# Down products of a gated feed-forward block: from plain block products to seven products of 2x2 blocks

## The chip, the cores and the metric

The kernel runs on one core of a Trainium2 chip. The metric is the device time of one execution, in microseconds (us). The engines are TensorE (PE, with its weight loads as PEld), VectorE (DVE), ScalarE (ACT), GpSimd (POOL) and SyncE (SP); SP and POOL start the DMAs. Each engine works through its own queue in order, and waits for others by semaphores.

## The reference

One inference step of a decoder of two layers, for 512 prompt tokens and 8 sample tokens that share the weights. Each layer has a feed-forward half-step, a mixer, and another half-step:

```
x = x + 1/2 * SwiGLU_a(RMSNorm(x))
x = x + Mixer(RMSNorm(x))       # layer 0: differential attention + gated linear attention; layer 1: mLSTM
x = x + 1/2 * SwiGLU_b(RMSNorm(x))
SwiGLU(x) = (silu(x @ w_gate) * (x @ w_up)) @ w_down      # 1024 -> 2816 -> 1024, all float32
```

So there are four half-steps, and the product with w_down in them is what is changed. The mixers' caches and states are outputs too; they are computed as before.

## The kernel before

The activations x lie feature by feature: 8 tiles of 128 features, each with 520 token columns, cut into two chunks, c0 of 256 and c1 of 264 columns (`CH`). A float32 product is made of three products of the faster type fp32r: `split` (L103) makes the high part by a cast on ACT (L105) and the low part by a subtraction on DVE (L106), and `dense` (L93) multiplies high weights by high x (L100), high by low x (L101) and low by high x (L102), for each block of 128x128 weights. Three matmuls per block and chunk, then.

The kernel is a row of stages: half-step, even mixer, half-step, half-step, odd mixer, half-step. `half_step` (L259) works through 2816 / 128 = 22 hidden tiles in GROUPS of 8, 7 and 7.

- The first four tiles (LEAD, function `early`, tiles g and u) are computed plainly while the norm and the combinations of x are still being made.
- The other 18 gate and up tiles use seven products of 2x2 blocks in place of eight (`product`): the 2x2 blocks are gate and up against the two halves of the 8 input tiles on the side of the weights, and the halves against the two chunks on the side of x. The products are p1, q5, p4 of the tile before, q6, p2, p3, p7, in that order, 4 blocks x 3 = 12 matmuls each, so 84 per tile. p1, q6, p7, p4 run into bank A, p2 into B, q5 and p3 into E. In between ACT evicts partial sums and DVE adds and multiplies them (L473 c<-B, L482 v<-E, L485 c<-A, L486, L490 c<-A). The results are split into hh and hl.
- The weights of such a tile come by SP in the tiles graw, u and raw (s); POOL adds blocks of w to s by an accumulating DMA (L426), and DVE adds graw and raw twice (L436). Then whi (ACT) and wlo (DVE) are made.
- At the end of a group its hidden tiles hh, hl are multiplied plainly by w_down: for each of 8 output tiles d and both chunks, the group's 8 or 7 blocks x 3 matmuls into a bank y, and DVE adds y to x (L558).
- In the last group of a half-step the last four d are taken chunk by chunk (lag = 4): four y of c0, then four y of c1, and between these the sum of squares (ACT sq, DVE acc, PE ss, DVE rs, PE bc) for the next stage's norm is put. The next stage's first products (pj in a mixer, g and u in a half-step) come behind them.

The order in each queue is fixed when the program is built, by a scheduler of the tile framework that takes the program's order and the priorities of marked blocks (`high_priority(AHF)`, for the weights). Pools of buffers decide the rest: three raw, two graw, one u2, five whi and wlo of the wide kind and two of the narrow kind, six PSUM banks.

Of the kernel before, what the change touches and what calls it, by code (L numbers as in the profile page):

```python
# [7 lines left out]
F32 = mybir.dt.float32  # L8
# [14 lines left out]
GROUPS = (8, 7, 7)  # L23
# [19 lines left out]
def ffn_order():  # L43

    out, f0 = [], 0
    for n in GROUPS:
        fs = range(f0, f0 + n)
        f0 += n
        for f in fs:
            out += [("g", f, k) for k in range(KT)] + [("u", f, k) for k in (4, 5, 6, 7, 0, 1, 2, 3)]  # L50
        for d in range(KT):
            out += [("d", d, f) for f in fs]
    return out


class Net:
# [101 lines left out]
    def norm_apply(self, c, ks, bc=None):  # L158
# [6 lines left out]
        for k in ks:  # L165
            q = self.tmp.tile([P, 264], F32, tag="xt", name="xt", bufs=3)
# [92 lines left out]
    def half_step(self, pos, first, last, xp, hp, pa):  # L259
# [122 lines left out]
        def early(f, w, c):  # L382
# [8 lines left out]
            h = f.h[:, s:s + n]  # L391
            if first:
                r = rms[c]
                v = small("v")[:, :n]
# [8 lines left out]
        def unit(u, gate):  # L403
            raw = (hp.tile([P, UNIT * P], F32, tag="graw", name="graw", bufs=2) if gate else
                   self.wraw.tile([P, UNIT * P], F32, tag="raw", name="raw"))
            self.wq.dma_start(out=raw, in_=self.t["w"][u])
            return raw

        def parts(src, n, names):

            tag = "" if n == 2 else "u"
            hi = self.whl.tile([P, n * H * P], F32R, tag=f"whi{tag}", name="whi", bufs=None if n == 2 else 2)
            lo = self.whl.tile([P, n * H * P], F32R, tag=f"wlo{tag}", name="wlo", bufs=None if n == 2 else 2)
            self.split(hi, lo, src)
            return {name: [(hi[:, i * P:i * P + P], lo[:, i * P:i * P + P]) for i in range(b * H, b * H + H)]
                    for b, name in enumerate(names)}

        def weights_gate(f):

            B = H * P  # L420
            f.g = unit(f.u0, True)
            f.u = hp.tile([P, B], F32, tag="u2", name="u2")
            self.wq.dma_start(out=f.u, in_=self.t["w"][f.u0 + 1, :, :B])
            f.s = self.wraw.tile([P, 2, B], F32, tag="raw", name="raw")
            self.wq.dma_start(out=f.s, in_=self.t["w"][f.u0 + 1, :, None, B:].to_broadcast([P, 2, B]))
            nc.gpsimd.dma_start(out=f.s, in_=self.t["w"][f.u0:f.u0 + 2, :, :B].rearrange("u p c -> p u c"),  # L426
                                accum_op=ALU.add)
            with tc.high_priority(AHF):
                f.w = parts(f.g, 2, ("g1", "g2"))

        def weights_rest(f):
            B = H * P
            g1, g2, s1 = f.g[:, :B], f.g[:, B:], f.s[:, 1, :]
# [3 lines left out]
            with tc.high_priority(AHF):  # L437
                f.w |= parts(f.u, 1, ("u2",))
                f.w |= parts(f.s.rearrange("p u c -> p (u c)"), 2, ("s3", "s1"))
                add(g1, s1)  # L440
                add(g2, g1)
                f.w |= parts(f.g, 2, ("s2", "s4"))

        class Hidden:
            def __init__(self, u0):
                self.u0 = u0
# [4 lines left out]
        def small(name):  # L451
            return hp.tile([P, n1], F32, tag=name, name=name, bufs=2)

        def product(kind, f, j):
            w, v = {"p1": ("g1", "x11"), "p2": ("g2", "x21"), "q5": ("s1", "a"), "q6": ("s2", "b"),
                    "p7": ("s3", "c"), "p3": ("s4", "x22"), "p4": ("u2", "d")}[kind]
            n = n0 if kind in ("p1", "p2", "p4") else n1
            new = kind in ("p1", "p2", "q5")
            if kind == "p1":
                f.A = bank("A")  # L460
            elif kind == "p2":
                f.B = bank("B")
            elif kind == "q5":
                f.E = bank("E")
            ps = f.B if kind == "p2" else f.E if kind in ("q5", "p3") else f.A
            self.dense(ps[:, :n], f.w[w], lambda k: tuple(q[:, :n] for q in ops[v](k)), ends=(new, True),
                       open_=kind != "p2")
            if kind == "p1":
                f.c1 = small("c1")
                self.evict(f.c1[:, :n0], ps[:, :n0])  # L470
            elif kind == "p2":
                g = f.c1[:, :n0]
                nc.vector.tensor_tensor(out=g, in0=ps[:, :n0], in1=g, op=ALU.add)  # L473
                nc.scalar.activation(g, g, AF.Silu)
            elif kind == "q5":
                f.c5 = small("c5")
                self.evict(f.c5, ps[:, :n1])
            elif kind == "q6":
                f.v = small("v")
                self.evict(f.v, ps[:, :n1])  # L480
            elif kind == "p3":
                nc.vector.tensor_tensor(out=f.v, in0=ps[:, :n1], in1=f.v, op=ALU.add)  # L482
                nc.scalar.activation(f.v, f.v, AF.Silu)
            elif kind == "p7":
                nc.vector.tensor_tensor(out=f.c5, in0=ps[:, :n1], in1=f.c5, op=ALU.add)  # L485
                nc.vector.tensor_tensor(out=f.v, in0=f.v, in1=f.c5, op=ALU.mult)  # L486
                self.split(hh[:, j, late], hl[:, j, late], f.v)
            elif kind == "p4":
                g = f.c1[:, :n0]
                nc.vector.tensor_tensor(out=g, in0=ps[:, :n0], in1=g, op=ALU.mult)  # L490
                self.split(hh[:, j, :n0], hl[:, j, :n0], g)
            step()

        u0 = pos // UNIT
        groups = []
        for nf in GROUPS:
            groups.append([Hidden(u0 + 2 * j) for j in range(nf)])
            u0 += 3 * nf
        leads = groups[0][:LEAD]
# [7 lines left out]
        while i < LEAD:  # L507
# [4 lines left out]
            for f in fs:  # L512
                f.h = hp.tile([P, T], F32, tag="h", name="h", bufs=LEAD)
# [9 lines left out]
        for gi, (nf, fs) in enumerate(zip(GROUPS, groups)):  # L523
            order = []
            for j in range(LEAD if gi == 0 else 0, nf):
                order += [("gate", j), ("rest", j), ("p1", j), ("q5", j)] + [("p4", j - 1)] * (j > (LEAD if gi == 0 else 0))
                order += [("q6", j), ("p2", j), ("p3", j), ("p7", j)]
            order.append(("p4", nf - 1))
            hh = hl = None
            for kind, j in order:  # L530
                if hh is None and kind in ("p7", "p4"):
                    hh = hp.tile([P, max(GROUPS), T], F32R, tag="hh", name="hh")
                    hl = hp.tile([P, max(GROUPS), T], F32R, tag="hl", name="hl")
                    if gi == 0:
# [1330 lines left out]
```

## Time and profile before

| | |
|---|---|
| time of the kernel before | 2206.93 us, median of 3 runs (2199.34 to 2207.18) |
| profiled execution | 2204.89 us, of it 2203.0 us from the first to the last instruction |
| mean granted clock of TensorE | 0.993 of full speed |
| busy: PE, PEld, DVE, ACT, POOL | 2157.5, 2044.5, 1418.3, 1015.2, 132.6 us |
| matmuls | 18340 |

Busy time is the union of the records of an engine. Matmuls overlap in the array, so that a record (some 0.28 us) says how long one takes, and the step from start to start how many go through in a time. A name such as y stands for all buffers of that name; `out<-in` gives what an instruction writes and reads, then its shape.

### The profile page before, as it was taken

Reading aid. Unit: us, or ns where it says so; the run is one execution under the profiler, and the core shown is the slowest. Engines: PE = TensorE matmul, PEld = TensorE weight load, DVE = VectorE, ACT = ScalarE, POOL = GpSimd, SP = SyncE. Lnnn points to the kernel's source line nnn. Section 1 sums busy time; section 2 is a strip of 40 time slices with the busy share of each in tenths; the row PEclk is TensorE's granted clock in tenths of the full one; section 3 lists DMA queues with packets and bytes.
Section 4 is the critical chain, followed back from the end, with each engine's and each line's share of the span. In section 5 each row is a group of like instructions: output and inputs, shape, how many; then the busy total and the mean of one; then the engine's idle time right before and its main releaser. Section 6 shows DMA issues by size and latency. Waiting matters only on the chain. (4 is left out here: it accounts for less than half of the span.)

```text
span 2203.0 us, 45950 instructions
## 1 busy us (share of the span) xinstructions
PE 2157.5 (98%) x18340; PEld 2044.5 (93%) x18340; DVE 1418.3 (64%) x3017; ACT 1015.2 (46%) x1932; POOL 132.6 (6%) x184
## 2 busy tenths in 40 slices
PE   8999999999999999999999999999999899999999
PEld 8999999876777899999999999999899899999999
DVE  8847475544486687475767566667655688648473
ACT  6636263334523455263645444454555555526261
POOL 1010101000000100101000000100000000000000
PEclk9999999999999999999999999999999999999999
DMA  7455544577787754555634555632545565555552
GB/s 226 138 127 166 135 134 140 161 262 260 237 274 240 258 145 141 123 170 124 175 97 120 156 141 150 149 100 89 159 149 158 151 194 171 143 130 158 144 135 78
DMA packets 146188, 352.94 MB, mean 160 GB/s; under 512 B 14433, under 2 KB 19090, under 8 KB 145846
## 3 DMA queue, kind: packets, MB, share of 16 engines
q1 hardware_dynamic: 113088, 273.79, 38.6%
q0 software_dynamic: 27120, 63.18, 14.5%
q10 hardware_dynamic: 5766, 13.05, 1.6%
q8 instruction: 144, 2.36, 0.4%
q14 instruction: 70, 0.57, 0.1%
HBM read 332.84 MB, written 17.11 MB: 159 GB/s over the span
## 5 line engine op out<-in xcount | busy, mean ns | idle before, releaser
L105 ACT CAST whi<-raw 128x1024 fp32r<-128x1024 f32 (+1 forms) x368 | 307.8, 840 | 345.6 <-PE y L101 178.9
L106 DVE TENSOR_TENSOR wlo<-raw,whi 128x1024 fp32r<-128x1024 f32 (+1 forms) x368 | 354.1, 967 | 145.9 <-ACT whi L105 139.9
L101 PE MATMUL y<-hl,whi 128*128 128x256 f32 (+1 forms) x1408 | 398.0, 283 | 0.0
L100 PE MATMUL y<-hh,whi 128*128 128x256 f32 (+1 forms) x1408 | 397.1, 283 | 0.0
L102 PE MATMUL y<-hh,wlo 128*128 128x256 f32 (+1 forms) x1408 | 396.9, 282 | 0.0
L100 PE MATMUL pj<-xh,whi 128*128 128x264 f32 (+1 forms) x896 | 261.2, 292 | 4.9 <-ACT whi L105 2.0
L101 PEld LDWEIGHTS y<-hl,whi 128*128 128x128 f32 x1408 | 265.1, 188 | 0.1
L100 PEld LDWEIGHTS y<-hh,whi 128*128 128x128 f32 x1408 | 264.8, 188 | 0.3
L102 PEld LDWEIGHTS y<-hh,wlo 128*128 128x128 f32 x1408 | 264.8, 188 | 0.0
L101 PE MATMUL pj<-xl,whi 128*128 128x264 f32 (+1 forms) x896 | 255.9, 286 | 0.0
L102 PE MATMUL pj<-xh,wlo 128*128 128x264 f32 (+1 forms) x896 | 255.2, 285 | 0.1
L101 PE MATMUL A<-xb,whi 128*128 128x264 f32 (+1 forms) x864 | 246.0, 285 | 0.0
L100 PE MATMUL A<-xb,whi 128*128 128x264 f32 (+1 forms) x864 | 244.8, 283 | 0.0
L102 PE MATMUL A<-xb,wlo 128*128 128x264 f32 (+1 forms) x864 | 244.7, 283 | 0.0
L105 ACT CAST whi<-graw 128x1024 fp32r<-128x1024 f32 x144 | 151.2, 1050 | 194.8 <-PE y L101 108.9
L106 DVE TENSOR_TENSOR wlo<-graw,whi 128x1024 fp32r<-128x1024 f32 x144 | 176.0, 1222 | 56.8 <-ACT whi L105 56.8
L558 DVE SCALAR_TENSOR_TENSOR x<-y,x 128x256 f32<-128x256 f32 (+1 forms) x192 | 81.9, 427 | 201.1 <-PE y L102 200.5
L100 PEld LDWEIGHTS pj<-xh,whi 128*128 128x128 f32 x896 | 170.8, 191 | 20.0 <-issue 9.1
L101 PEld LDWEIGHTS pj<-xl,whi 128*128 128x128 f32 x896 | 170.9, 191 | 3.4 <-issue 3.3
L102 PEld LDWEIGHTS pj<-xh,wlo 128*128 128x128 f32 x896 | 170.6, 191 | 1.9 <-issue 1.4
L100 PE MATMUL E<-xh,whi 128*128 128x264 f32 x576 | 163.8, 284 | 0.5 <-ACT c L586 0.5
L100 PEld LDWEIGHTS A<-xb,whi 128*128 128x128 f32 x864 | 162.7, 188 | 1.3
(469 smaller groups left out, 5168.2 us busy)
## 6 DMA issues: line engine op xcount, KB each, us to landing
raw<-w SPq DMA_DIRECT2D x240, 512.0 KB, 3.7
raw<-w POOLq DMA_DIRECT2D x112, 512.0 KB, 6.0
graw<-w SPq DMA_DIRECT2D x72, 512.0 KB, 4.8
kt<-ckt SPq DMA_DIRECT2D x128, 256.0 KB, 4.6
vtile<-cv SPq DMA_DIRECT2D x128, 256.0 KB, 4.2
u<-w SPq DMA_DIRECT2D x72, 256.0 KB, 3.0
cs<-sc SPq DMA_DIRECT2D x16, 512.0 KB, 5.3
kb<-kqd SPq DMA_DIRECT2D x16, 512.0 KB, 6.9
```

The costliest lines, as they stand in the source:

```text
L100: nc.tensor.matmul(ps, lhsT=wh, rhs=xh, start=(ends[0] and i == ks[0]), stop=False, skip_group_check=open_)
L101: nc.tensor.matmul(ps, lhsT=wh, rhs=xl, start=False, stop=False, skip_group_check=open_)
L102: nc.tensor.matmul(ps, lhsT=wl, rhs=xh, start=False, stop=(ends[1] and i == ks[-1]), skip_group_check=open_)
L105: self.nc.scalar.copy(out=hi, in_=src)
L106: self.nc.vector.tensor_tensor(out=lo, in0=src, in1=hi, op=ALU.subtract)
L558: nc.vector.scalar_tensor_tensor(xs, y[:, :n], -0.5, xs, ALU.mult, ALU.add)
```

## The change

GROUPS becomes 6, 6, 6 and 4. The down products of the first three groups, 18 of the 22 tiles, are now also made with seven products of 2x2 blocks; the last group of 4 stays plain. A `Down` is such a unit. Its blocks are: pairs of hidden tiles (three pairs in a group, the sum over k), pairs of outputs (d and d + 4) and the two chunks. So a group has 4 Downs, of 7 products x 3 pairs x 3 = 63 matmuls. Their weights come and are combined as those of a gate tile, in sizes of 768 and 384 columns instead of 1024 and 512. Each product that ends a partial sum is added to x by DVE (L552), six additions per Down: two of E (264 columns), two of A (264), one of A and one of B (256).

A pair of hidden tiles is gathered in a tile `h` of four slots of 264 columns (tag stg, one buffer; the second pair of leads lies in a graw buffer), whose unused last 8 columns POOL sets to zero. When both tiles are there, `combine` makes the differences (L468 of 528 columns, L471 and L472 of 264) and splits all seven operands into hh and hl (792, 528 and 528 columns).

The Downs of a group don't stand at its end: they come behind the first gate tile of the next group. And p1 of a unit is now copied by ACT from bank A to bank B, where p2 adds to it, in place of the addition c<-B on DVE. Buffers: squares sq 4 to 3, xt 3 to 2, c5 2 to 1.

```diff
-GROUPS = (8, 7, 7)
+GROUPS = (6, 6, 6, 4)
...
+        class Pair:
+            def open(self, tag="stg"):
+                if self.h is None:
+                    self.h = hp.tile([P, 4 * n1], F32, tag=tag, name="h",
+                                     bufs=2 if tag == "graw" else None).rearrange("p (s t) -> p s t", s=4)
+                    nc.gpsimd.memset(self.h[:, 0:3:2, n0:], 0.0)
...
+            def parts(self, a, b, j):
+                self_split(hidden[0][:, self.i, j:j + b - a], hidden[1][:, self.i, j:j + b - a], self.h[:, a:b])
+
+            def combine(self):
+                x11, x22, x21, x12 = [self.h[:, i] for i in range(4)]
+                cm = hp.tile([P, 4 * n1], F32, tag="cmb", name="cmb").rearrange("p (s t) -> p s t", s=4)
+                nc.vector.tensor_tensor(out=cm[:, 0:2], in0=self.h[:, 0:2], op=ALU.subtract,
+                                        in1=x12[:, None, :].to_broadcast([P, 2, n1]))
+                self.parts(0, 3, 0)
+                nc.vector.scalar_tensor_tensor(cm[:, 2], cm[:, 1], -1.0, x11, ALU.mult, ALU.subtract)
+                nc.vector.scalar_tensor_tensor(cm[:, 3], cm[:, 2], -1.0, x21, ALU.mult, ALU.subtract)
+                for a in (0, 2):
+                    self_split(hidden[0][:, self.i, 3 + a:5 + a], hidden[1][:, self.i, 3 + a:5 + a], cm[:, a:a + 2])
...
+        class Unit:
+            def product(f, kind):
+                w, v = WHERE[kind]
+                n = n0 if kind in ("p1", "p2", "p4") else n1
+                if kind == "p1":
+                    f.A, f.B = bank("A"), bank("B")
+                elif kind == "q5":
+                    f.E = bank("E")
+                ps = f.B if kind == "p2" else f.E if kind in ("q5", "p3") else f.A
+                self.dense(ps[:, :n], f.w[w], lambda k: tuple(q[:, :n] for q in f.rhs(v, k)), ends=(kind in ("p1", "q5"), True),
+                           open_=True)
+                if kind == "p1":
+                    self.evict(f.B[:, :n0], ps[:, :n0])
+                f.out(kind, ps[:, :n])
+                step()
...
+        class Down(Unit):
...
+            def out(f, kind, ps):
+                if kind == "p1":
+                    return
+                row = 0 if kind in ("q6", "p2", "p3") else 1
+                cols = slice(0, n0) if kind in ("p2", "p4") else late
+                xs = x[:, f.d + row * H, cols]
+                nc.vector.scalar_tensor_tensor(xs, ps, row - 0.5, xs, ALU.mult, ALU.add)
...
+                seq += fs[:1] + downs + fs[1:]
...
+        for f in seq:
+            weights(f)
+            f.product("p1")
+            f.product("q5")
+            if before is None:
...
+                for p in (leads[0].pair, leads[2].pair):
+                    p.combine()
+            else:
+                before.product("p4")
...
+            for kind in ("q6", "p2", "p3", "p7"):
+                f.product(kind)
+            before = f
+        before.product("p4")
```

How this stands in the queues, at three places. First VectorE where the first down products of the kernel begin. Before, the last gate tile of the first group (c, v, hl) is followed by updates x<-y with a low part of weights now and then:

```order
L490 TENSOR_TENSOR c_2567<-A,c_2567 128x256
L106 TENSOR_TENSOR hl<-v,hh 128x264
L106 TENSOR_TENSOR wlo<-u_3201,whi 128x512
L106 TENSOR_TENSOR hl<-c_2567,hh 128x256
L558 SCALAR_TENSOR_TENSOR x<-y,x 128x256
L558 SCALAR_TENSOR_TENSOR x<-y,x 128x264
L558 SCALAR_TENSOR_TENSOR x<-y,x 128x256
L106 TENSOR_TENSOR wlo<-raw,whi 128x1024
L558 SCALAR_TENSOR_TENSOR x<-y,x 128x264
```

Now the same queue in the first group's second and third Down (A_1292, and A_1390 with B_1391 and E_1402), whose updates stand between the low parts of the next units' weights (768 columns for a Down, 1024 for a gate tile) and their sums:

```order
L552 SCALAR_TENSOR_TENSOR x_69<-E_1402,x_69 128x264
L432 TENSOR_TENSOR graw_1463<-graw_1463 128x384
L552 SCALAR_TENSOR_TENSOR x_69<-A_1292,x_69 128x256
L112 TENSOR_TENSOR wlo_1475<-u2_1465,whi_1474 128x384
L552 SCALAR_TENSOR_TENSOR x_69<-A_1390,x_69 128x264
L552 SCALAR_TENSOR_TENSOR x_69<-B_1391,x_69 128x256
L112 TENSOR_TENSOR wlo_1485<-graw_1463,whi_1484 128x768
L552 SCALAR_TENSOR_TENSOR x_69<-E_1402,x_69 128x264
L112 TENSOR_TENSOR wlo_1569<-graw_1561,whi_1568 128x1024
L112 TENSOR_TENSOR wlo_1577<-raw_1565,whi_1576 128x1024
L432 TENSOR_TENSOR graw_1561<-graw_1561,raw_1565 128x512
L552 SCALAR_TENSOR_TENSOR x_69<-A_1390,x_69 128x264
```

Between two updates of one bank there are now other instructions of up to 1024 columns.

Second, VectorE behind the plain tiles of the first half-step. Before, the four lead tiles (h) are split while the first seven-product tiles run (c5<-A_795 is the first one's p7):

```order
L436 TENSOR_TENSOR graw_1031<-graw_1031,raw_1035 128x512
L106 TENSOR_TENSOR hl_877<-h_164,hh_876 128x520
L436 TENSOR_TENSOR graw_1031<-graw_1031 128x512
L106 TENSOR_TENSOR hl_877<-h_165,hh_876 128x520
L106 TENSOR_TENSOR hl_877<-h_516,hh_876 128x520
L106 TENSOR_TENSOR wlo_1053<-graw_1031,whi_1052 128x1024
L106 TENSOR_TENSOR hl_877<-h_659,hh_876 128x520
L485 TENSOR_TENSOR c5_825<-A_795,c5_825 128x264
```

Now both pairs of leads (h_163 in the stage tile and h_515) are combined and split there, and c5<-A_794 is the first p7:

```order
L472 SCALAR_TENSOR_TENSOR cmb_834<-cmb_834,h_163 128x264
L432 TENSOR_TENSOR graw_1032<-graw_1032,raw_1036 128x512
L112 TENSOR_TENSOR hl_833<-h_515,hh_832 128x792
L112 TENSOR_TENSOR wlo_1048<-raw_1036,whi_1047 128x1024
L432 TENSOR_TENSOR graw_1032<-graw_1032 128x512
L112 TENSOR_TENSOR hl_833<-cmb_834,hh_832 128x528
L521 TENSOR_TENSOR h_866<-E_811,h_866 128x264
L468 TENSOR_TENSOR cmb_844<-h_515 128x528
L112 TENSOR_TENSOR wlo_1054<-graw_1032,whi_1053 128x1024
L471 SCALAR_TENSOR_TENSOR cmb_844<-cmb_844,h_515 128x264
L112 TENSOR_TENSOR hl_833<-cmb_844,hh_832 128x528
L472 SCALAR_TENSOR_TENSOR cmb_844<-cmb_844,h_515 128x264
```

In front of the first p7 there are more and longer instructions than before.

Third, TensorE at the end of the first half-step, where the even mixer's projections (pj) begin. Before, three of their matmuls stand in front of ss, the last piece of the sum of squares of c1:

```order
L100 MATMUL y<-hh,whi 128x264
L101 MATMUL y<-hl,whi 128x264
L102 MATMUL y<-hh,wlo 128x264
L100 MATMUL pj<-xh,whi 128x256
L101 MATMUL pj<-xl,whi 128x256
L102 MATMUL pj<-xh,wlo 128x256
L154 MATMUL ss<-ones,acc 128x1 x3
L100 MATMUL pj<-xh,whi 128x256
```

Now sixteen stand there; this is the end of them:

```order
L106 MATMUL pj<-xh,whi 128x256
L107 MATMUL pj<-xl,whi 128x256
L108 MATMUL pj<-xh,wlo 128x256
L106 MATMUL pj<-xh,whi 128x256
L160 MATMUL ss<-ones,acc 128x1 x3
L107 MATMUL pj<-xl,whi 128x256
```

Thirteen matmuls of pj have moved in front of ss.

## Rows read from the trace of the kernel before

**Rows 1.** Head of the page: the span, and busy time of each engine.

```profile
span 2203.0 us, 45950 instructions
PE 2157.5 (98%) x18340; PEld 2044.5 (93%) x18340; DVE 1418.3 (64%) x3017; ACT 1015.2 (46%) x1932; POOL 132.6 (6%) x184
```

**Rows 2.** Groups by line and shape, plain down matmuls: busy, mean ns, idle before.

```profile
L100 PE MATMUL y<-hh,whi 128*128 128x256 f32 x704 | 198.9, 283 | 0.0
```

**Rows 3.** Timeline of PE, plain down products: start, duration, engine, line, instruction.

```profile
357.84 0.28 PE L100 MATMUL y<-hh,whi 128*128 128x256 f32 x1
...
358.78 0.28 PE L102 MATMUL y<-hh,wlo 128*128 128x256 f32 x1
358.89 0.28 PE L100 MATMUL y<-hh,whi 128*128 128x264 f32 x1
...
360.97 0.28 PE L102 MATMUL y<-hh,wlo 128*128 128x264 f32 x1
```

**Rows 4.** Windows, a stretch of gate and up tiles; columns as named.

```profile
core 0: us, PE busy (x) PEld busy (x) DVE busy (x) ACT busy (x) POOL busy (x), PEclk, DMA share, GB/s
935.00:990.00 55.00, 55.00 (x459) 55.00 (x458) 43.02 (x71) 33.80 (x61) 2.36 (x2) 1.00 0.61 171
```

**Rows 5.** Timeline of DVE, one gate and up tile; idle before in brackets.

```profile
940.71 0.42 DVE L473 TENSOR_TENSOR c<-B,c 128x256 f32<-128x256 f32 x1 [1.31 <-PE B L102]
941.73 1.22 DVE L106 TENSOR_TENSOR wlo<-graw,whi 128x1024 fp32r<-128x1024 f32 x1 [0.59 <-ACT whi L105]
942.87 0.42 DVE L482 TENSOR_TENSOR v<-E,v 128x264 f32<-128x264 f32 x1
943.21 1.22 DVE L106 TENSOR_TENSOR wlo<-graw,whi 128x1024 fp32r<-128x1024 f32 x1
...
945.88 0.69 DVE L436 TENSOR_TENSOR graw<-graw,raw 128x512 f32<-128x512 f32 x1
946.48 0.43 DVE L486 TENSOR_TENSOR v<-v,c 128x264 f32<-128x264 f32 x1
...
950.83 0.42 DVE L473 TENSOR_TENSOR c<-B,c 128x256 f32<-128x256 f32 x1 [1.31 <-PE B L102]
```

**Rows 6.** Groups by line and shape on DVE and ACT.

```profile
L106 DVE TENSOR_TENSOR wlo<-raw,whi 128x1024 fp32r<-128x1024 f32 x192 | 234.4, 1223 | 49.9 <-ACT whi L105 49.6
...
L106 DVE TENSOR_TENSOR wlo<-raw,whi 128x512 fp32r<-128x512 f32 x176 | 119.8, 687 | 96.0 <-ACT whi L105 90.3 <-PE trs L642 2.2 <-PE pj L102 2.0
...
L473 DVE TENSOR_TENSOR c<-B,c 128x256 f32<-128x256 f32 x72 | 30.5, 424 | 105.5 <-PE B L102 105.2
...
L105 ACT CAST whi<-graw 128x1024 fp32r<-128x1024 f32 x144 | 151.2, 1050 | 194.8 <-PE y L101 108.9
```

**Rows 7.** DMA issues: KB each, median us from issue to landing.

```profile
raw<-w SPq DMA_DIRECT2D x240, 512.0 KB, 3.7
raw<-w POOLq DMA_DIRECT2D x112, 512.0 KB, 6.0
```

**Rows 8.** Windows, the ends of the first three half-steps; columns as in rows 4.

```profile
370.30:374.30 4.00, 0.06 (x2) 0.00 (x1) 3.64 (x14) 1.47 (x4) 2.00 (x4) 0.85 0.69 190
374.30:380.30 6.00, 6.00 (x29) 5.95 (x29) 1.82 (x12) 0.00 (x0) 0.00 (x0) 0.53 0.75 248
...
1160.00:1164.00 4.00, 2.56 (x20) 2.17 (x19) 2.81 (x8) 1.61 (x4) 0.00 (x0) 1.00 0.06 23
1506.00:1512.00 6.00, 3.82 (x29) 3.20 (x27) 6.00 (x18) 4.79 (x12) 0.54 (x2) 1.00 0.01 3
```

**Rows 9.** Windows, the start of the first half-step; columns as in rows 4.

```profile
50.00:60.00 10.00, 10.00 (x85) 10.00 (x84) 10.00 (x19) 6.26 (x9) 1.17 (x1) 1.00 0.60 137
60.00:70.00 10.00, 10.00 (x85) 10.00 (x84) 10.00 (x14) 7.78 (x15) 0.00 (x0) 1.00 0.35 107
70.00:80.00 10.00, 10.00 (x85) 10.00 (x84) 9.73 (x15) 5.58 (x9) 0.00 (x0) 1.00 0.36 106
80.00:90.00 10.00, 9.52 (x80) 9.31 (x79) 8.22 (x18) 6.77 (x13) 0.00 (x0) 1.00 0.41 123
```

More of the change, by code (lines that the diff above doesn't have):

```diff
@@ L414, in parts @@
             self.split(hi, lo, src)
-            return {name: [(hi[:, i * P:i * P + P], lo[:, i * P:i * P + P]) for i in range(b * H, b * H + H)]
+            return {name: [(hi[:, i:i + P], lo[:, i:i + P]) for i in range(b * B, b * B + B, P)]
                     for b, name in enumerate(names)}
[L418 to L429, printed above, removed]
@@ L437, in weights_rest @@
             with tc.high_priority(AHF):
[L438 to L446, printed above, removed]
+                f.w = parts(g, B, 2, ("g1", "g2"))
+                f.w |= parts(u, B, 1, ("u2",))
+                f.w |= parts(s, B, 2, ("s3", "s1"))
@@ L448, in bank @@
+                add(g[:, :B], s[:, B:])
+                add(g[:, B:], g[:, :B])
+                f.w |= parts(g, B, 2, ("s2", "s4"))
         def bank(name):
             return pa.tile([P, 512], F32, tag="acc", name=name)
[L451 to L492, printed above, removed]
@@ new lines, in half_step @@
+        u0 = pos // UNIT
+        seq, gates = [], []
+        for gi, nf in enumerate(GROUPS):
+            plain = gi == len(GROUPS) - 1
+            pairs = [Pair(i, plain) for i in range(nf // 2)]
+            fs = [Gate(u0 + 2 * j, pairs[j // 2], j % 2) for j in range(nf)]
+            gates += fs
+            u0 += 2 * nf
+            if gi == 0:
+                seq += fs
+            else:
+                seq += fs[:1] + downs + fs[1:]
+                if plain:
+                    fs[0].late = True
+            if not plain:
+                downs = [Down(u0 + 2 * d, d, nf // 2) for d in range(H)]
+                u0 += 2 * H
@@ new lines, in half_step @@
+        before = None
+        for f in seq:
[3 more added lines that the diff above has]
+            if before is None:
+                while steps:
+                    step()
+                hidden += [hp.tile([P, max(GROUPS) // 2, 7, n1], F32R, tag=n, name=n) for n in ("hh", "hl")]
+                for p in (leads[0].pair, leads[2].pair):
+                    p.combine()
+            else:
+                before.product("p4")
+                if isinstance(before, Down) and before is downs[-1]:
+                    p = gates[-GROUPS[-1]].pair
+                    p.parts(0, 1, 0)
+                    p.parts(3, 4, 3)
+            for kind in ("q6", "p2", "p3", "p7"):
+                f.product(kind)
+            before = f
@@ L1710, in ffn_tiles @@
     out = []
[L1711 to L1712 removed]
+    for o in ffn_order():
+        out.append(np.zeros((P, P), np.float32) if o is None else b[o[0]][o[2], o[1]])
     return out
```

194 lines of the change are left out of this document (112 added, 82 removed).

## The prediction

> **What bounds the kernel now.** I read the head of the page first. What it shows is that TensorE is busy in 98% of the span, VectorE in 64% and ScalarE in 46% [rows 1]: TensorE sets the time nearly everywhere, and a change that takes matmuls away can pay only while the others still feed it. Then I asked what one matmul is worth. By its record it lasts 283 ns [rows 2], but records overlap: the starts of the timeline step by 0.1175 us for 256 columns (357.84 to 358.78 is eight steps) and by 0.122 us for 264 (358.89 to 360.97 is seventeen steps) [rows 3], and a window of 55 us without a pause holds 459 matmuls, 0.120 us each [rows 4]. Steps, not records, are what an instruction costs here. Last I read VectorE in the same window, because the change moves work to it. In the gate and up tiles it is already busy 43 of 55 us [rows 4], and one tile of them, 940.71 to 950.83, 10.12 us, has 1.31 and 0.59 us in which it waits [rows 5]; the other 8.22 us (81%) are work, one instruction behind the other.
>
> **What is removed.** Per half-step the 22 plain tiles took 22 x 8 outputs x 2 chunks x 3 = 1056 down matmuls. Now twelve Downs of 7 x 3 x 3 = 63 and a plain group of 4 x 8 x 2 x 3 = 192 take 948. That is 108 less in each of four half-steps, 432 in all, and all of 256 columns: those of 264 are 528 per half-step before, and 12 x 36 + 96 = 528 after. 432 x 0.1175 = 50.8 us [rows 3]. By records it would be 122 us, which is the number to avoid. At the mean step of 0.120 it would be 51.8, so this term is sure within 1 us as long as TensorE stays fed.
>
> **What VectorE gets, in its steady stretches.** An instruction's slot is the distance to the next start: 1.14 us for 1024 columns (941.73 to 942.87), 0.60 for 512 (945.88 to 946.48), 0.34 for 264 (942.87 to 943.21) [rows 5]. In between by line (1.05 ns a column) I estimate 0.87 us for 768, 0.46 for 384, 0.89 for 792, 0.62 for 528.
> A Down has three low parts of 768, one of 384, two weight sums of 384 and six updates of x: 2.61 + 0.46 + 0.92 + 2.04 = 6.0 us. TensorE needs 36 x 0.122 + 27 x 0.1175 = 7.6 us for it. So VectorE is at 80% there, where plain down products left it far below.
> A pair of gate tiles loses the addition c<-B (72 of them before [rows 6]) and the two hl of each tile, 6 x 0.34 = 2.04, and gets the combinations and their low parts: 0.62 + 0.89 + 2 x 0.62 + 2 x 0.34 = 3.43. So 2 x 8.22 - 2.04 + 3.43 = 17.8 us stand against 2 x (48 x 0.122 + 36 x 0.1175) = 20.2 us of TensorE, 88%. ScalarE gets more casts and the copy B<-A, but had 46% [rows 1] and takes part of the removed work away too; I cost it at nothing, TensorE's products hiding it; without that cover a late cast of 768 columns would hold a product by up to its own length, an estimated 0.8 us from the 1050 ns of 1024 columns [rows 6]. The loads and the POOL accumulations (3.7 and 6.0 us to landing [rows 7]) stay under three raw buffers, so up to two units of 7.6 us or more ahead; 48 more accumulations and the small zero fills go into POOL's queue, which was busy 6% [rows 1]. Costed at nothing as well; if that cover went, a late weight sum would hold one product by some of the 6.0 us.
>
> **Where the chains are tight.** x<-A of p7 must have read its bank before p4 writes there. TensorE gives 9 + 9 + 9 steps after the end of p3: 1.10 + 1.06 + 1.10 = 3.26 us. In the order VectorE may have x<-E, two low parts of 768 and a sum of 384 ahead of x<-A: 0.34 + 2 x 0.87 + 0.46 and its own 0.42 [rows 6] are 2.96. It fits by 0.3 us. Where the next low parts are a gate tile's, as before x<-A_1390 in the piece of the order, it is 0.34 + 2 x 1.14 + 0.60 + 0.42 = 3.64, over by 0.4; that comes once per group, 12 times, 5 us for the borders (bounds 0, if these low parts run earlier, and 15, if more is late; before, the borders cost nothing that could be won). At a pair's end the only stage tile is given on: after p4 come the product, a subtraction of 264, a low part of 512, another 264, low parts of 528 and 792 (0.34 + 0.34 + 0.60 + 0.34 + 0.62 + 0.89 = 3.13), then ScalarE's eviction of the next q6, 0.4; TensorE gives q6, p2, p3, 24 x 0.122 + 12 x 0.1175 = 4.34 us. It fits by some 0.8 less the handshakes. There are 7 such hand-overs in a half-step, 28 in all. I take 0.2 us for each, 6 us (bounds 0 and 28 x 1; a gain is excluded, since there was no such hand-over).
>
> **The ends of the half-steps.** The next norm is hidden behind four y of chunk 1. These had 4 x 21 x 0.122 = 10.3 us, now 4 x 12 x 0.122 = 5.9, so 4.4 us less at each of three ends (the fourth is the kernel's end). Before, the end at 370 lost 3.94 us, and then 6 us at a granted clock of 0.53 of full speed (the 1.2 GHz level) with 29 matmuls, where 50 would fit: 2.5 us more; the end at 1160 lost 1.44 and the one at 1506 2.18 us [rows 8]. Now the order puts sixteen projection matmuls ahead of ss instead of three, 1.5 us of new cover, so the first end loses 2.9 more; for the other two I take 0.9 and 2.2, 6 us together. Bounds: all cover shows, 3 x 4.4, and the slow stretch comes at two more ends, 2 x 2.5, so +18; or the slow stretch goes, -2.5.
>
> **The start of the first half-step.** VectorE is at 10.00, 10.00, 9.73 and 8.22 of 10 us from 50 to 90, and TensorE lost 0.48 us there [rows 9]. Four hl of 520 (0.61 each) leave, two combinations of 3.43 come: 4.4 us more in a stretch without room. The order also shows the next tile's eviction waiting for the first combination, since it needs the one stage tile. I take 6 us (bounds 0 and 12; nothing here can gain). The other half-steps start with their combinations made earlier.
>
> **Sum.** 2204.9 (the profiled execution) - 50.8 + 6 (ends) + 6 (first start) + 6 (hand-overs) + 5 (borders) = 2177 us. That execution lies 2 us under the median of 2206.93, which is less than I can resolve.
>
> **A rule against the change.** Row: the low part that starts at 941.73 and lasts 1.22 us would end at 942.95, but its successor starts at 942.87, 0.08 us earlier [rows 5]. The Trainium skill, "VectorE: DVE Perf Modes", section "The DRAIN you can't avoid", says that after every operation the pipe empties before the next one starts. Under that rule whole records would add up: by rows, with 955 ns for 768 columns and 553 for 384 by line between 687 and 1223 [rows 6], a Down is 7.1 of 7.6 us and a pair 18.8 of 20.2; then the second rival below is what one would forecast. The same page's section on two instructions with no wait between them lets a successor that isn't held start earlier, and here the trace agrees with that one: the 0.08 us stand in every pair without a dependence.
>
> **Rivals.** First, nothing is given back: the cover is long enough everywhere. 2204.9 - 50.8 = 2154. For it speaks that every chain above fits on paper; against it that VectorE at 50 to 90 has no room at all.
> Second, VectorE limits the gates. Before it waited 1.90 us per tile for products. If 1.5 of these stay per tile, because it runs in order and the products come when they come, a pair takes 17.8 + 3.0 = 20.8 and loses 0.6 us, 36 pairs 22 us: 2204.9 - 50.8 + 6 + 6 + 5 + 22 = 2193. For it speaks the 88%; against it that the waits of before were there because TensorE was late, and shrink when VectorE is.
> Third, and slower: the reads before writes in the Downs. Both x<-A must be done before p7 and p4. If at each of these two places one subtraction of 512 or more (0.60 us) stands ahead beyond the margin, a Down loses 1.2 us, 48 Downs 58: 2177 + 58 = 2235. The change turns into a loss from (2204.9 - 2177) / 48 = 0.6 us per Down on. For it speaks the margin of 0.3 us; against it that the order spreads most low parts between the updates.
> That the change doesn't remove the matmuls can't be: they are counted in the order. A larger gain than 51 us would have to come out of the 45 us in which TensorE was idle [rows 1], most of them in the mixers that aren't touched.
>
> **How the numbers follow.** Forecast (2162 to 2186) 0.47; nothing given back (2150 to 2162) 0.17; VectorE limits (2186 to 2206) 0.20; the Downs' reads (2206 and more, some just below) 0.11; below 2150 0.05. Half a per cent, 11 us, is about what a measurement here tells from no change: faster is below 2196. Faster: 0.47 + 0.17 + 0.05 + 0.11 of the second rival = 0.80. Same: 0.09 of the second and 0.02 of the third = 0.11. Slower: 0.09. The range of 2152 to 2206 leaves out about 0.1 on either side.
>
> **What would show it.** Right: 63 matmuls of a Down in about 7.6 us without a gap, and A, E and B of the gates as dense as in [rows 4]; VectorE near 80% in the Downs and near 88% in the gates; pauses of TensorE of 2 to 6 us around the first combinations and of some 3 us more at the end near 370. Wrong: TensorE pausing regularly before p7 or p4 with VectorE's x as the releaser (third rival), or before p7 of each pair's successor with ScalarE's h (hand-overs dearer than 0.2 us), or VectorE without gaps through whole gate stretches (second rival). A granted clock at half in more places than the one at 374 would also break the sum.

## The result and the profile after

The changed kernel takes 2192.35 us (median of 4 executions, 2189.03 to 2195.87) against 2205.43 us of the kernel before on the same chips. The ratio is 0.9937, with a 95% interval of 0.9920 to 0.9954: faster, by 13 us where 28 were forecast. 432 matmuls are gone as counted; of the 50.8 us that they are worth at [rows 3], some 38 came back as delays.

The head of the page of the profiled execution (2194.01 us), to be read against [rows 1]:

```profile
span 2192.2 us, 46399 instructions
PE 2130.5 (97%) x17908; PEld 2001.1 (91%) x17908; DVE 1629.2 (74%) x3409; ACT 1108.1 (51%) x2080; POOL 194.6 (9%) x276
```

TensorE has 432 matmuls less (18340 before), but its busy time fell by 27.0 us only, and its idle time rose from 45.5 to 61.7 us. Part of the loss sits inside "busy", since a record of 0.28 us covers a delay of up to 0.16 us behind a step of 0.12. So I measured delays by steps: for each matmul of 256 or 264 columns, the time to the next matmul's start less 0.1175 or 0.122 us, summed over a stretch. This sum is called excess below; matmuls slowed by a lower granted clock count in it too.

Windows of the profile after: 972 to 996 lies in the Downs of one group, 1008 to 1058 in gate tiles. Columns as in [rows 4]:

```profile
972.00:996.00 24.00, 23.98 (x200) 23.76 (x199) 20.71 (x37) 11.32 (x16) 3.56 (x3) 1.00 0.76 190
1008.00:1058.00 50.00, 50.00 (x414) 49.65 (x413) 42.54 (x68) 31.11 (x53) 7.18 (x9) 1.00 0.69 161
```

200 matmuls in 24 us are 0.120 each, and 414 in 50 us are 0.121: the Downs and the gates run as dense as [rows 4]. VectorE is busy 86% and 85% by records there. So it does not set the pace in the steady stretches.

The starts are another matter. Windows of 42 us from the first gate product of each half-step, first those of the kernel before, then those after:

```profile
58.70:100.70 42.00, 41.52 (x343) 41.20 (x342) 37.47 (x59) 28.21 (x50) 0.00 (x0) 1.00 0.43 132
837.90:879.90 42.00, 42.00 (x350) 41.89 (x349) 33.72 (x53) 25.74 (x44) 0.00 (x0) 1.00 0.45 134
1197.50:1239.50 42.00, 42.00 (x350) 41.89 (x349) 33.75 (x53) 25.71 (x44) 0.00 (x0) 1.00 0.44 134
1889.30:1931.30 42.00, 42.00 (x350) 41.89 (x349) 33.74 (x53) 25.69 (x44) 0.00 (x0) 1.00 0.43 133
...
59.00:101.00 42.00, 36.70 (x285) 35.76 (x284) 36.74 (x60) 23.05 (x41) 3.75 (x5) 0.96 0.46 110
842.20:884.20 42.00, 39.70 (x325) 38.99 (x324) 35.98 (x59) 22.91 (x40) 4.94 (x6) 1.00 0.55 136
1200.80:1242.80 42.00, 39.28 (x321) 38.59 (x320) 35.79 (x59) 22.99 (x40) 4.96 (x6) 1.00 0.57 134
1885.30:1927.30 42.00, 39.51 (x323) 38.82 (x322) 36.16 (x59) 23.14 (x40) 4.94 (x6) 1.00 0.56 132
```

58, 25, 29 and 27 matmuls fewer fit, at 0.12 us each 7.0, 3.0, 3.5 and 3.2 us; by excess it is the same: 8.1, 3.3, 3.7 and 3.5 us, where it was 1.1, 0.3, 0.3 and 0.3. In the first of them some of that is clock (0.96 granted against 1.00). What the second half-step waits for is in the timeline of all engines, rows of the second gate tile and the third one's weights:

```profile
850.41 1.22 DVE L112 TENSOR_TENSOR wlo<-graw,whi 128x1024 fp32r<-128x1024 f32 x1
851.54 0.43 DVE L472 SCALAR_TENSOR_TENSOR cmb<-cmb,h 128x264 f32<-128x264 f32 x1
851.65 1.44 SPq L423 DMA_DIRECT2D graw<-w  x2
...
856.57 1.05 ACT L111 CAST whi<-graw 128x1024 fp32r<-128x1024 f32 x1 [2.91 <-DMA graw<-w]
857.53 1.05 ACT L111 CAST whi<-raw 128x1024 fp32r<-128x1024 f32 x1
857.65 1.23 DVE L112 TENSOR_TENSOR wlo<-graw,whi 128x1024 fp32r<-128x1024 f32 x1 [3.23 <-ACT whi L111]
858.48 0.61 ACT L111 CAST whi<-u 128x512 fp32r<-128x512 f32 x1
859.00 0.38 ACT L655 ACTIVATE c<-E 128x264 f32<-128x264 f32 x1
...
859.43 0.39 PE L106 MATMUL E<-xh,whi 128*128 128x264 f32 x1 [0.91 <-ACT c L655]
```

Two graw loads start half a us apart: at 851.65, when the last wlo of the former gate tile has read graw (850.41 + 1.22), and at 852.10, when the combination of the second lead pair has read its h (851.54 + 0.43), which lies in the other graw buffer. ScalarE sits at a cast that waits for the first of them; behind the cast, in order, stands c<-E, which TensorE's p3 needs. VectorE, named in many of the later waits, was idle for 3.23 us before. That the first load would have started earlier with both buffers in the ring is a reading of these rows; the run with a lead buffer of its own, below, tests it.

The first half-step's start has a late graw load too. Its longest wait is this one, and ScalarE makes the h that TensorE waits for only behind the cast:

```profile
72.86 1.04 ACT L111 CAST whi<-graw 128x1024 fp32r<-128x1024 f32 x1 [2.42 <-DMA graw<-w]
...
76.52 0.59 PE L106 MATMUL A<-xb,whi 128*128 128x264 f32 x1 [3.55 <-ACT h L655]
```

At a group's border the timeline shows the case for which the prediction had 0.4 us, here at the last Down: its p4 starts at 909.77, once its p7 update x<-A is done (909.29 + 0.42). TensorE's step from 909.39 to 909.77 is 0.38 us instead of 0.12:

```profile
904.33 2.36 DVE L112 TENSOR_TENSOR wlo<-graw,whi 128x1024 fp32r<-128x1024 f32 x2 [0.51 <-ACT whi L111]
...
906.61 1.22 DVE L112 TENSOR_TENSOR wlo<-raw,whi 128x1024 fp32r<-128x1024 f32 x1
907.74 0.68 DVE L432 TENSOR_TENSOR graw<-graw,raw 128x512 f32<-128x512 f32 x1
908.35 0.42 DVE L552 SCALAR_TENSOR_TENSOR x<-E,x 128x264 f32<-128x264 f32 x1
908.69 0.68 DVE L432 TENSOR_TENSOR graw<-graw 128x512 f32<-128x512 f32 x1
909.29 0.42 DVE L552 SCALAR_TENSOR_TENSOR x<-A,x 128x264 f32<-128x264 f32 x1
909.39 0.28 PE L107 MATMUL A<-xb,whi 128*128 128x264 f32 x1
...
909.77 0.39 PE L106 MATMUL A<-hh,whi 128*128 128x256 f32 x1
```

Last the ends. At the second one the kernel before went on 0.1 us behind the last y and lost 1.44 us some 12 us later, near 1160 [rows 8]. After:

```profile
1145.00:1149.00 4.00, 1.30 (x10) 0.92 (x8) 3.61 (x10) 2.54 (x6) 0.00 (x0) 0.89 0.42 135
1149.00:1159.00 10.00, 10.00 (x49) 10.00 (x50) 7.68 (x27) 2.61 (x7) 0.00 (x0) 0.53 0.16 51
1159.00:1169.00 10.00, 10.00 (x83) 9.72 (x82) 7.13 (x22) 3.61 (x9) 0.00 (x0) 1.00 0.01 2
```

TensorE stands for 2.7 of 4 us, and then runs 49 matmuls in 10 us at a granted clock of 0.53 (1.2 GHz for most of it), 83 in the next 10 us at full clock. The third end lost 2.18 us at full clock before [rows 8]; now it has several short waits and then a slow stretch as well. The end near 370, on the other hand, lost 3.94 us and a slow stretch before [rows 8]; now its delays are waits of up to half a us between the projections, at full clock, and together about as long. After, first end and third end:

```profile
366.00:372.00 6.00, 5.00 (x33) 3.87 (x32) 5.72 (x21) 3.23 (x8) 2.85 (x5) 1.00 0.98 282
...
1505.00:1512.00 7.00, 4.19 (x26) 3.08 (x24) 7.00 (x20) 5.65 (x14) 0.60 (x2) 1.00 0.01 1
1512.00:1518.00 6.00, 5.63 (x34) 5.63 (x35) 5.46 (x19) 1.54 (x4) 0.00 (x0) 0.72 0.60 171
```

By excess from 28 us before the last y to 30 us behind it, the three ends went from 6.5, 2.6 and 4.0 us to 6.9, 8.1 and 7.1: 9.1 us more.

### The profile page after: what moved, and what is told of

It reads as the page before. It is cut to its first block, busy times and chain, and to the rows that moved or that the text cites. A ratio compares the mean times of both kernels' runs of the same rounds, so it can differ in the third digit from the quotient of the medians.

```text
span 2192.2 us, 46399 instructions
## 1 busy us (share of the span) xinstructions
PE 2130.5 (97%) x17908; PEld 2001.1 (91%) x17908; DVE 1629.2 (74%) x3409; ACT 1108.1 (51%) x2080; POOL 194.6 (9%) x276
## 3 DMA queue, kind: packets, MB, share of 16 engines
q0 software_dynamic: 40176, 82.05, 20.9%
## 4 chain that ended last, share of the span: by engine, by line
PE 74%; DVE 13%; DMA 9%; ACT 3%; issue 2%; SPq 0%; ACTq 0%; DVEq 0%; POOLq 0%
PE A L106 9%; PE A L108 8%; PE A L107 8%; PE E L106 4%; PE E L107 4%; PE E L108 4%; DVE wlo L112 4%; PE pj L106 4%; PE pj L108 3%; PE pj L107 3%; PE y L106 2%; DMA raw<-w 2%; PE y L107 2%; PE y L108 2%; PE B L108 2%; PE B L107 2%
## 5 line engine op out<-in xcount | busy, mean ns | idle before, releaser
L112 DVE TENSOR_TENSOR wlo<-raw,whi 128x512 fp32r<-128x512 f32 (+2 forms) x344 | 311.9, 910 | 106.1 <-ACT whi L111 101.6
L111 ACT CAST whi<-raw 128x512 fp32r<-128x512 f32 (+2 forms) x344 | 273.2, 799 | 153.8 <-PE pj L107 76.6
L112 DVE TENSOR_TENSOR wlo<-graw,whi 128x1024 fp32r<-128x1024 f32 (+1 forms) x240 | 266.4, 1115 | 113.3 <-ACT whi L111 112.2
L111 ACT CAST whi<-graw 128x1024 fp32r<-128x1024 f32 (+1 forms) x240 | 231.2, 965 | 154.4 <-PE B L107 90.0
L106 PEld LDWEIGHTS A<-xb,whi 128*128 128x128 f32 x864 | 163.4, 189 | 13.4 <-DVE c L524 5.9
L106 PE MATMUL A<-hh,whi 128*128 128x264 f32 (+1 forms) x576 | 165.5, 287 | 2.0
L107 PEld LDWEIGHTS A<-xb,whi 128*128 128x128 f32 x864 | 163.1, 189 | 0.8 <-DVE xb L112 0.8
L107 PE MATMUL E<-xl,whi 128*128 128x264 f32 x576 | 163.4, 284 | 0.0
L108 PEld LDWEIGHTS A<-xb,wlo 128*128 128x128 f32 x864 | 163.3, 189 | 0.0
L108 PE MATMUL E<-xh,wlo 128*128 128x264 f32 x576 | 163.2, 283 | 0.0
L107 PE MATMUL A<-hl,whi 128*128 128x264 f32 (+1 forms) x576 | 162.7, 282 | 0.0
```

What stands on the lines that cost most here:

```text
L106: nc.tensor.matmul(ps, lhsT=wh, rhs=xh, start=(ends[0] and i == ks[0]), stop=False, skip_group_check=open_)
L107: nc.tensor.matmul(ps, lhsT=wh, rhs=xl, start=False, stop=False, skip_group_check=open_)
L108: nc.tensor.matmul(ps, lhsT=wl, rhs=xh, start=False, stop=(ends[1] and i == ks[-1]), skip_group_check=open_)
L111: self.nc.scalar.copy(out=hi, in_=src)
L112: self.nc.vector.tensor_tensor(out=lo, in0=src, in1=hi, op=ALU.subtract)
```

## The experiments

Each was timed beside the kernel before. Single executions of one kernel spread over 7 to 15 us, so medians a few us apart decide nothing by themselves; the excess by stretch, read from each trace, repeats within some tenths of a us where the granted clock is full, and only within some us where it isn't. "The middle" of a half-step is the stretch from 42 us behind its first gate product to 28 us before its last y.

**Two stage buffers.** The short diff, on the changed kernel:

```diff
-hi = self.whl.tile([P, n * H * P], F32R, tag=f"whi{tag}", ..., bufs=None if n == 2 else 2)
+hi = self.whl.tile([P, n * H * P], F32R, tag=f"whi{tag}", ..., bufs=None if n == 2 else 1)   # lo alike
-    self.h = hp.tile([P, 4 * n1], F32, tag=tag, name="h", bufs=2 if tag == "graw" else None)
+    self.h = hp.tile([P, 4 * n1], F32, tag=tag, name="h", bufs=2)
-f.pair.open("stg" if i < 2 else "graw")
+f.pair.open()
```

> The changed kernel with two stage buffers for pairs of hidden tiles, and both lead pairs in them instead of the second one in a graw buffer; to make room, the narrow whi and wlo (the u2 block) have one buffer instead of two. In the changed kernel's trace, TensorE's steps between 842 and 884 hold 3.3 us more than their nominal sum (0.3 before), 3.7 and 3.5 in the third and fourth half-step, 8.1 in the first; from 854.4 to 857.7 VectorE waits for ScalarE and that for a graw load issued only at 851.65. Theory, the lent buffer: the second lead pair holds one of two graw buffers until its combination, so the gates' weights pass through the other one alone and come late. Then all of these excesses fall below 1.5 us, the wait for graw goes, and the small stalls of 0.18 us at each pair's hand-over go too: 3 x 2 + 5 + 28 x 0.18 = 16 us, a time of about 2176. Rival, VectorE is full at the starts because of the combinations: the excesses stay above 2.5 us each and the time within 5 us of the changed kernel's 2192.

Measured: 2185.29 us, ratio 0.9896 (0.9872 to 0.9920). The windows of the first three starts:

```profile
58.90:100.90 42.00, 39.52 (x310) 38.73 (x309) 39.46 (x65) 25.18 (x44) 5.07 (x7) 0.96 0.47 113
836.00:878.00 42.00, 41.62 (x343) 41.03 (x342) 37.85 (x63) 23.78 (x40) 5.05 (x7) 1.00 0.54 129
1189.50:1231.50 42.00, 41.61 (x342) 41.03 (x341) 37.83 (x63) 23.79 (x40) 5.07 (x7) 1.00 0.59 134
```

The excesses fell to 1.2 us in the second to fourth half-step and to 5.1 in the first, although VectorE does all its combinations there (its busy time in the windows even rises). The rival is out for those three; the first still waits for a stage (1.8 us before p7 with ScalarE's h as releaser). The 0.18 us at a pair's hand-over went inside the groups, but a new delay of 0.25 us came once per group, and the middle's excess fell only from 14.8 to 13.4 us. Of the 16 us that the theory promised, about half came.

**The control for the room.** One buffer for the narrow parts, and nothing else (the first two lines of the diff above).

> The changed kernel with one buffer instead of two for the narrow whi and wlo alone, the control for the room that the stage buffers took. Both theories: no difference, within 4 us of 2192, since u2 is used by p4, a whole unit (7.6 us or more) before the next one is needed. If it is slower by more than that, the run with two stage buffers has to be read against this one.

Measured: 2193.64 us, 0.9930 (0.9909 to 0.9952). No difference, as expected: the 8.3 us between it and the run above are the stage buffers'.

**The lead pair alone.** The stage stays single, the second lead pair gets a buffer of its own (with the control's room):

```diff
-    self.h = hp.tile([P, 4 * n1], F32, tag=tag, name="h", bufs=2 if tag == "graw" else None)
+    self.h = hp.tile([P, 4 * n1], F32, tag=tag, name="h", bufs=None)
-f.pair.open("stg" if i < 2 else "graw")
+f.pair.open("stg" if i < 2 else "lead")
```

> The changed kernel with one stage buffer as it has, but the second lead pair in a buffer of its own instead of a graw buffer (and one buffer for the narrow whi and wlo, for the room). It tells the two places apart that the run with two stage buffers changed together. Theory, the lent graw buffer makes the starts of the second to fourth half-step late in the changed kernel (in the kernel before, where it was given back 8 us earlier, lending cost nothing): their excess in the first 42 us falls from 3.3 to 3.7 us to about 1.2, as with two stage buffers, and the middle of the half-steps stays at 3.6; 7 us below the control, about 2187. Rival, the single stage buffer is the cause there too: these excesses stay above 2.5 us and the time within 3 us of 2193.

Measured: 2184.86 us, 0.9902 (0.9887 to 0.9917). The starts:

```profile
59.90:101.90 42.00, 39.67 (x308) 38.74 (x308) 39.58 (x65) 25.17 (x44) 3.75 (x5) 0.96 0.46 109
839.70:881.70 42.00, 41.62 (x342) 41.09 (x341) 37.73 (x63) 23.80 (x40) 5.05 (x7) 1.00 0.55 128
```

The excess is 1.2 us in the three later starts and 5.2 in the first; the middle stays at 3.5 us per half-step. So in the three later starts it is the graw buffer, not the stage. The first start won 2.9 us by it too (8.1 to 5.2), some of it perhaps by the clock: the control for the room, which lends graw as the changed kernel does, has 6.3 there.

**Lending in the kernel before.**

```diff
-f.h = hp.tile([P, T], F32, tag="h", name="h", bufs=LEAD)
+f.h = (hp.tile([P, UNIT * P], F32, tag="graw", name="h", bufs=2)[:, :T] if f is leads[2] else
+       hp.tile([P, T], F32, tag="h", name="h", bufs=LEAD))
```

> The kernel before, in which the third lead tile's h lies in a graw buffer until it is split into hh and hl, as the second lead pair does in the changed kernel; nothing else. It is given back near 843 in the second half-step, some 8 us earlier than in the changed kernel. Theory, the lent buffer by itself makes the second gate's weights late: TensorE's excess in the first 42 us behind the first gate product rises from 0.3 us to 1 to 3 us in the second to fourth half-step and from 1.1 in the first, 4 to 12 us in all, a time of about 2214. Rival, the starts of the changed kernel are late for the combinations on VectorE alone: excesses and time as before, within 3 us of 2206.

Measured: 2205.36 us, 0.9999 (0.9987 to 1.0010), excess 0.3 us in the later starts as before. The second start, with the 350 matmuls of the kernel before:

```profile
837.10:879.10 42.00, 42.00 (x350) 41.89 (x349) 33.71 (x53) 25.32 (x44) 0.00 (x0) 1.00 0.49 146
```

My expectation missed: lending by itself costs nothing where the tile is split early. In the changed kernel the combination that frees it ends near 852, and by these two runs only lending and late return together are dear.

**Without the Downs' weight sums.** VectorE's additions in the Downs are left out (the output is another, as the expectation says):

```diff
+if isinstance(f, Gate):
     add(g[:, :B], s[:, B:])
     add(g[:, B:], g[:, :B])
```

> The changed kernel without the two additions of graw and raw in the Downs (0.93 us of VectorE per Down; these weights are then left uncombined, and the output is another). VectorE's share in the Downs falls from about 80% to 68%. Theory, in the middle of the half-steps VectorE costs only where it stands in front of one update: the excess behind the third Down (0.36 us per group) and little else goes, 3 to 5 us in all, about 2188. Rival, VectorE limits the Downs: 48 x 0.5 us and more, 2168 or less.

Measured: 2193.03 us, 0.9931 (0.9912 to 0.9951). The middle's excess went from 3.8, 3.7, 3.6, 3.7 to 3.3, 3.2, 3.3, 3.3 us, 1.7 us in all. VectorE does not limit the Downs; less was won than the 3 to 5 us of the theory.

**The short last group by itself.** The kernel before, `GROUPS = (6, 6, 6, 4)`.

> The kernel before, all down products plain, with its groups cut 6, 6, 6, 4 as in the change and nothing else. It has as many matmuls as before (18340). What the shorter last group costs by itself: theory, the cover of 5.9 instead of 10.3 us at three ends loses 4.4 us at each and lets the granted clock fall at one or two of them: 10 to 18 us slower than before, about 2219. Rival, the ends of the changed kernel are slow for its other work (fewer squares and xt buffers, VectorE fuller): within 4 us of the kernel before.

Measured: 2216.74 us, 1.0043 (1.0027 to 1.0060): 9.2 us slower, 6 to 13 by the interval, just under the 10 to 18 expected. Windows of its first two ends:

```profile
370.00:374.00 4.00, 0.82 (x7) 0.62 (x6) 4.00 (x12) 2.43 (x7) 2.99 (x6) 0.91 0.57 192
374.00:384.00 10.00, 7.48 (x34) 7.10 (x34) 5.40 (x26) 3.09 (x6) 0.94 (x2) 0.52 0.53 183
...
1153.00:1157.00 4.00, 1.30 (x10) 0.92 (x9) 3.63 (x9) 2.75 (x6) 0.00 (x0) 1.00 0.44 137
1157.00:1167.00 10.00, 10.00 (x59) 9.90 (x59) 7.29 (x24) 2.40 (x6) 0.00 (x0) 0.66 0.14 52
```

The same pause as in the changed kernel (1.30 of 4 us busy at the second end) stands in a kernel whose down products are all plain. The second end loses for the group's length. The first end is not the same: here TensorE pauses for some 6 us behind the last y and then runs at half clock, which the changed kernel, with its sixteen projection matmuls ahead of ss, doesn't. Between this kernel and the changed one lie 24.4 us by the medians (23 by the two ratios): about what the seven products are worth beside a short last group. The terms worked out below, 50.8 less 7.0 and 9.6 for the starts and 9.8 for the middle, also give 24.4; that they agree to the tenth is luck, as the medians are known to some 3 us only.

**Six outputs chunk by chunk.** `lag = 0 if last else 6` in place of 4.

> The changed kernel with six instead of four outputs taken chunk by chunk at the end of a half-step, so that c1 has six y of 12 matmuls, 8.8 us, behind c0's last one instead of 5.9. In the changed kernel's trace the end at 1146 loses 2.9 us waiting for xh, and then some 40 matmuls run with 0.096 us more each (granted clock at 1.2 GHz), 4 us. Theory, too short a cover: both go, and the time is 5 to 8 us shorter, about 2186. Rival, the next norm's chain on VectorE and ScalarE is limited by its own work, not by where c0's last y stands: the pause at the second end stays above 2 us and the time within 3 us of 2192.

Measured: 2193.20 us, 0.9936 (0.9914 to 0.9957). In the trace the pause at the second end went from 3.0 to 0.1 us and no slow stretch follows, but the median did not move. By itself this run settles nothing. With two stage buffers as well:

> Two stage buffers (both lead pairs in them, one buffer for the narrow whi and wlo) and six outputs chunk by chunk at the end of a half-step, on the changed kernel. The stage buffers alone gave 2185.3, the six outputs alone 2193.2, the changed kernel 2192.4. Theory, cover and lent buffer are separate losses: the pause of 3.0 us between the second and the third half-step goes to 0.1 us in the trace as it did with the six outputs alone, the granted clock doesn't fall there, and the time is 3 to 7 us below the stage buffers' alone, about 2180. Rival, the end's cover is not worth anything in the mean of the runs (the six outputs alone didn't move the median): 2185, within 3 us.

Measured: 2184.11 us, 0.9897 (0.9877 to 0.9916): the pause is gone (0.1 us), the median is within 1.2 us of the stage buffers' alone. By the time the rival held. The traces say in part why six outputs bring so little. The excess of the three ends is 22.1 us in the changed kernel, but 18.0 to 19.1 in the four other runs with four outputs (two stage buffers, the control, the lead buffer, no weight sums), which met less slow clock at the second end. With six it is 16.8 and 17.9: the second end falls to 2.8 and 2.7 us, but the third one rises to 8.2 and 8.0, from 6.3 to 7.1 with four. By these traces six outputs are worth 1 to 2 us. Why the third end gets worse is open.

**Eight outputs**, `lag = 0 if last else 8`, without and with the stage buffers:

> The changed kernel with all eight outputs chunk by chunk at the end and nothing else (no second stage buffer). Theory, cover and buffers are separate losses that add: with two stage buffers eight instead of four outputs gave 2173.7 against 2185.3, 11.6 us, so here 2192 - 11 = about 2181, with the pause between the second and third half-step at 0.1 us and less time at the low granted clock. Rival, most of those 11.6 us were executions that happened to meet fewer stretches of low clock: 2188 or more.

Measured: 2184.79 us, 0.9909 (0.9894 to 0.9924), 7.6 us under the changed kernel (6 by the two ratios), between the two expectations. The excess of the three ends is 14.8 us.

> As the run with stage buffers and six outputs, but with all eight outputs chunk by chunk, so that c1's cover at the end is 8 x 12 x 0.122 = 11.7 us, more than before the change (10.3). Four wide whi and wlo are then held at once, of five. Theory, with the cover of before the ends cost what they did before: 6 to 10 us below the stage buffers' alone (the short last group alone cost 9.2 us), about 2177. Rival, holding four of five weight buffers delays the next stage's weights: the pause moves to the first products behind the end, and the time is 2185 or more.

Measured: 2173.70 us, 0.9860 (0.9840 to 0.9881). It beats both kernels, by 18.7 and 31.6 us, and by 11.6 the stage buffers alone, more than the 6 to 10 expected. The excess of its three ends is 13.9 us, near the 13.0 of the kernel before. Its second end:

```profile
1130.00:1134.00 4.00, 4.00 (x35) 3.86 (x34) 4.00 (x11) 2.45 (x6) 0.00 (x0) 1.00 0.59 205
1134.00:1144.00 10.00, 9.86 (x85) 9.66 (x83) 9.17 (x32) 2.19 (x6) 0.00 (x0) 1.00 0.18 54
```

85 matmuls in 10 us at full clock stand where the changed kernel had 49.

**Five outputs in the kernel before**, `lag = 5`.

> The kernel before with five outputs chunk by chunk at the end instead of four, which is all that its five weight buffers hold: c1's cover becomes 5 x 21 x 0.122 = 12.8 us. It asks whether the kernel before loses at its ends for want of cover too (3.9 and 2.5 us near 370, 2.2 near 1506). Theory, cover: the pause near 370 shrinks by 2.5 us and the low clock after it may go, 3 to 6 us faster, about 2201. Rival, all five buffers held delay the next stage's weights: as before or slower, 2205 to 2212.

Measured: 2196.24 us, 0.9967 (0.9952 to 0.9983): 9 us faster (4 to 11 by the interval), more than the 3 to 6 expected; the excess of the three ends fell from 13.0 to 7.0 us. The kernel before lacked cover too, and of the 31.6 us above, this much could be had without the change.

## Why the prediction was half right

The forecast was 2177 us, 28 less than before; 13 came. Part by part:

- What is removed: right. 432 matmuls left the trace, and the steady stretches step by 0.120 and 0.121 us.
- VectorE's load in steady stretches: right in what follows from it. I forecast 80% and 88% in slots, the windows show 86% and 85% in records, which overlap a little; no loss hangs on it. The second rival came out near the measured time (2193), but that is chance, since its mechanism isn't there: leaving work out of VectorE gave 1.7 us of excess.
- Hand-overs and borders: right in size. I put 6 + 5 us; the excess in the middle of the four half-steps rose from 5.0 to 14.8 us, 9.8 (about 11.5, if the middle is taken up to the first y of the last group in both). The single delays are 0.18 us at a hand-over (0.2 forecast), and 0.3 and 0.36 us at the last two Downs of a group (0.4 forecast, once per group; it comes twice).
- The third rival, reads before writes in every Down: wrong. Only the Downs at a border wait.
- The start of the first half-step: right in size, 7.0 us of excess more against 6, and partly by luck. My mechanism was a full VectorE and the one stage tile. The stage wait is there (1.8 us are left with the lead buffer), but up to 2.9 of the 7.0 us went with the lent graw buffer, and during the longest wait VectorE stood idle until 73.94, for 2.3 us, waiting for ScalarE.
- The step that failed is the sentence behind it: "The other half-steps start with their combinations made earlier." I costed these starts at nothing. They cost 3.0, 3.4 and 3.2 us, 9.6 in all. I had seen that the second lead pair is put in a graw buffer, and followed the stage buffer only; the graw ring, with two buffers for the loads of 4.2 us that it feeds, was not walked with one. The run with a lead buffer of its own shows it.
- The ends: the mechanism was right, the term was too small, and it sat at the wrong ends. I had 2.9, 0.9 and 2.2 us, 6 in all; the changed kernel's trace has 0.4, 5.5 and 3.1, 9.1 in all, and the short last group by itself costs 9.2 (6 to 13). I let the slow clock come at no new end. It came at the second and the third, and left the first. How much of it comes varies: the four other runs with four outputs have 5.0 to 6.1 us more than the kernel before.

With the measured terms the sum is 2204.9 - 50.8 + 7.0 + 9.6 + 9.8 + 9.1 = 2189.6, against a median of 2192.35 and 2194.0 in the profiled execution. Most of what is missing in the latter stands at a place that the prediction had no term for: the plain tiles in front of the second half-step, with 2.9 us of excess more. There TensorE waits 2.25 us for the sum of squares instead of 1.53 and then runs at half clock, with 29 matmuls in 6 us where the kernel before had 49:

```profile
794.00:800.00 6.00, 6.00 (x29) 6.00 (x29) 4.86 (x15) 2.53 (x3) 0.00 (x0) 0.50 0.55 181
```

The prediction's last sign of being wrong, a granted clock at half in more places than the one at 374, came true.

The low part that starts at 906.61 would end at 907.83, and its successor starts at 907.74, 0.09 us earlier. So after the change too whole records don't add up, as the rule weighed in the prediction would have them do (the Trainium skill, "VectorE: DVE Perf Modes", "The DRAIN you can't avoid": the next operation starts when the pipe is empty). The pair fits the exception which the same section of the Trainium skill makes: a next operation that is not held starts earlier.

## What to carry to other kernels

When a change lends a buffer of a ring to something else, walk that ring with one buffer less until the borrower's last reader: what is late first is the load, then whatever stands behind its consumer in an in-order queue. Shortening the last block of a stage shortens the cover of the next stage's start; price it by what stands there now, and where a new pause arises, count in the stretch at the lower clock that stood behind such pauses in the traces (0.53 granted at the second end here). And measure delays by the steps of a pipelined engine, since its busy time hides those shorter than a record.

## What the runs showed of the hardware

The granted clock fell also away from the places that the edits aim at. From the last y of the third half-step to the first product of the fourth, the odd mixer, the profiled executions took 332.8 us (before), 330.3 (changed), 340.3 (control for the room), 336.6 (two stage buffers) and 328.5 (the last version). Summed over slices of 2 us with a granted clock below 0.95, the share of speed not granted while TensorE was busy comes to 12.9, 15.6, 22.4, 20.9 and 9.3 us in the whole of these executions. The same goes for executions of one kernel: of 17 of the kernel before, timed beside one another, the fastest took 2198.3 us at a mean granted clock of 0.996 and the slowest 2210.1 at 0.990, which is 9 and 22 us not granted. In most of the other groups time and clock go together like this, though not in the six of the lead buffer. So a spread of 10 us between executions of one kernel is mostly the clock, and runs of single profiles must not be compared by their spans at this size.
